# A hybrid decoder layer on one core: w_out loaded in two halves of its columns, and the first weight sums of the gated MLP on VectorE

## The chip, the cores and the metric

The kernel runs on one core of one Trainium2 chip. The metric is device time in microseconds, the median of three runs. The core has four engines that compute: TensorE (PE) for matmuls and transposes, VectorE (DVE), ScalarE (ACT) and GpSimd (POOL); SyncE (SP) issues the transfers. Each engine takes its instructions in the order in which they stand in its queue, and an instruction that waits holds all that stands behind it.

## What is computed

One layer on x of 1024 tokens by 1024 channels, in float32:

```python
h = rms_norm(x, norm_mix_pre)
proj = h @ w_in
a_out = spatial_gating(ua, va, ...)            # 256 channels
b_out = dilated_attention(qb, kb, vb, rel_bias) # 12 heads of 64
mix = concatenate([a_out, b_out], -1)
x = x + rms_norm(mix @ w_out, norm_mix_post)
h = rms_norm(x, norm_ffn_pre)
g = gelu(causal_dwconv(h @ w_gate, conv_w, conv_b))
y = (g * (h @ w_up)) @ w_down
x = x + rms_norm(y, norm_ffn_post)
```

The change touches the product with `w_out` (1024 by 1024), the end of the attention heads that stand before it, and the start of the gated MLP behind it.

## The kernel before

**Pairs of fp32r.** TensorE multiplies in a reduced float32 format. A value is therefore split into a high part (a cast) and a low part (value minus cast), and a product is three matmuls: high by high, low by high, high by low. `split(hi, lo, src, e1, e2)` makes the two parts, the cast on engine e1 (line 73 on ScalarE, line 77 on VectorE), the subtraction on e2 (line 78, VectorE or GpSimd).

**Heads.** The twelve heads run one after the other, each in four groups g. `qk_row` makes a row of scores (matmuls into `s`, the bias and minimum on VectorE, Exp on ScalarE at line 547, the scaling by 1/z on GpSimd at line 550). `tpv` transposes the rows (`pt`), takes them apart into `pth` (ScalarE, line 574) and `ptl` (VectorE, line 575), and multiplies them by V into `o`; `last` adds `o` into the mix tile `mixN` (lines 604, 605). Between these, `pump` takes matmuls from the deque `fill`, so that TensorE has work while the other engines prepare a group: in heads 0 to 9 they project Q and K of a later head (`proj_qk`), in the last head (h = 11) they are the first products with w_out.

**w_out.** `load_wo(k)` loads 128 rows of w_out (512 KB) into one of two raw buffers and splits them in two halves of 512 columns into `wohK` and `wolK`. The eight tiles are loaded during head 10 by `WO_AT`; the strings `WO_HI` and `WO_LO` name the engines of casts and subtractions. A raw buffer comes free when the subtractions on it are done. `mix_split` splits the eight 128x128 blocks of one token tile of the mix (`ms`). `wout_mm(i, ks, get)` gives the matmuls of token tile i into two PSUM banks, `y_i_0` for the left 512 columns and `y_i_1` for the right. In the last head the fill is tile 0 with blocks k = 0 to 6 (42 matmuls); block 7 follows when the head is done, then come tiles 1 to 4, 6, 5, 7 in the order `TO`.

**Norms.** `wout_end(i)` closes a tile: two squares with sums on ScalarE (line 725), a root on ScalarE (161), a step on GpSimd (166), scaling by g2 on VectorE (729), the sum with x (730), a square on ScalarE (733), a root (150), a step on GpSimd (154), and the scaling `xb` on VectorE (735). `h2_trans` transposes the result (`hT`, line 747). The transposes of a tile stand behind the y matmuls of the next tile in TensorE's queue.

**MLP.** The products with w_gate and w_up are in seven products of 2x2 blocks (Strassen's), with sums of weight blocks (`tsums`: four subtractions of 128x512) and of activations (`hs_sums`), each split again (`hs`, `wtg`, `wtu`). `HEAD` gives the order of the first three units, a = gate 0, b = up 0, c = gate 1: "1a 1b 2a 1c 2b 2c 4a 6a 6b 7a ...". `wsplit` is written three products ahead (`LOOK`). `tsums` before puts its first and last subtraction on GpSimd (lines 824 and 827), the others on VectorE (825, 826). `TO[7]` = 7 is transposed at j = 4. The scheduler orders instructions by the order of the code and their readiness; `tc.high_priority(400)` lets those in it go ahead.

Of the kernel before, what the change touches and what calls it, by code (L numbers as in the profile page):

```python
# [26 lines left out]
R = mybir.dt.float32r  # L27
# [8 lines left out]
KT = D // 128  # L36
HEADS = 12
# [15 lines left out]
WQK_HI = 'aa'  # L53
WO_HI = 'dadaddda'
WO_LO = 'pppppppd'
WO_AT = {0: (0, 1), 1: (), 2: (2, 3), 3: (4, 5), 4: (6, 7)}
# [6 lines left out]
def build(tc, x, g1, g2, g3, g4, w_in, ln_g, ln_b, sp_w, sp_b, rel, w_out, w_gate, w_up,  # L63
# [28 lines left out]
    with tc.manual_schedule(engines={ET.PE, ET.SP}), \  # L92
# [530 lines left out]

        def load_wo(k):
            r = raw("wo%d" % k)
            sp.dma_start(r, w_out[k * 128:(k + 1) * 128, :])
            wh = htile("woh%d" % k)
            wl = htile("wol%d" % k)
            for s in (slice(0, 512), slice(512, 1024)):
                split(wh[:, s], wl[:, s], r[:, s], ENG[WO_HI[k]], ENG[WO_LO[k]])  # L630
            WO.append((wh, wl))

# [8 lines left out]

        def wout_mm(i, ks, get):
            def mm(hf, k, j):
                def f():
                    if k == 0 and j == 0:
                        YP[i, hf] = get("y%d_%d" % (i, hf))
                    m = MS[i][1 if j == 2 else 0][:, k]
                    w = WO[k][1 if j == 1 else 0][:, hf * 512:(hf + 1) * 512]
                    pe.matmul(YP[i, hf], m, w, start=k == 0 and j == 0, stop=k == KT - 1 and j == 2)  # L649
                return f  # L650
            return [mm(hf, k, j) for k in ks for hf in range(2) for j in range(3)]

# [6 lines left out]
        for h in range(HEADS):  # L659
# [6 lines left out]
            if h == HEADS - 1:  # L666
                pump(len(fill))
                fill.extend(wout_mm(0, range(KT - 1), bD))
            for g in range(4):
# [16 lines left out]
                if g == 3 and h == HEADS - 2:  # L686
                    pump(len(fill))
                    for k in WO_AT[4]:
                        load_wo(k)
        pump(len(fill))  # L690
        last_pv()
        close_pool("ag")
        close_pool("ag2")
# [129 lines left out]
        def tsums(u):  # L823
            pool.tensor_sub(tw(u, 0), wblk(u, 0, 1), wblk(u, 0, 0))  # L824
            dve.tensor_sub(tw(u, 1), wblk(u, 1, 1), tw(u, 0))
            dve.tensor_sub(tw(u, 2), wblk(u, 1, 1), wblk(u, 0, 1))
            pool.tensor_sub(tw(u, 3), wblk(u, 1, 0), tw(u, 1))

# [286 lines left out]
        load_xb(1)  # L1115
        for f in wout_mm(0, [KT - 1], bD):
            f()
        wout_end(0)
        mt = mix_tiles(1)
        mix_split(1, mt[0], mt[1], range(KT))  # L1120
        for c in range(1, NT):
# [7 lines left out]
            if c == 6:  # L1129
# [3 lines left out]
                hs_sums(0, 2)  # L1133
            for f in wout_mm(i, range(KT), bS if c % 2 else bD):
                f()
            if c < 6:
                wout_end(i)
            else:
                with tc.high_priority(400):
                    wout_end(i)  # L1140
# [16 lines left out]
        for j, (u, n) in enumerate(SEQ):  # L1157
# [5 lines left out]
            if j == 1:  # L1163
                with tc.high_priority(400):
                    h2_trans(TO[NT - 2], bD)
                store_x1(TO[NT - 2])
                tsums(U[0])
                hs_sums(2, 3)
                hsplit(4, 0, 3)
# [4 lines left out]
            if j == 4:  # L1174
                with tc.high_priority(400):
                    h2_trans(NT - 1, bD)
                store_x1(NT - 1)
                hsplit(4, 3, 4)
                hs_sums(3, 4)
                hsplit(6, 3, 4)  # L1180
                hsplit(7, 3, 4)
                tsums(U[1])
                hsplit(5, 0, 4)
                hsplit(3, 0, 4)
# [104 lines left out]
```

## Time and profile before

| | before |
|---|---|
| device time, median of 3 runs | 1190.84 us (1188.72 to 1192.52) |
| the profiled execution | 1192.9 us |
| its span | 1191.2 us |
| TensorE busy | 1162.8 us (98%) |
| VectorE busy | 832.0 us (70%) |
| ScalarE busy | 593.1 us (50%) |
| GpSimd busy | 351.0 us (29%) |

Times in the rows are microseconds from the start of the span. TensorE is the engine that is nearly always busy; of its 28 us without work 10.9 lie between 400 and 600 us, where head 10 ends at about 431, head 11 at about 458, the products with w_out at about 550, and the MLP begins. Idle time of the other engines costs nothing in itself.

### The profile page before, as it was taken

The numbers are of one execution on the slowest core, as the hardware profiler recorded it, in microseconds if no ns is written. First come the engines' busy times: TensorE is split into PE (matmuls) and PEld (weight loads), VectorE is DVE, ScalarE is ACT, GpSimd is POOL, SyncE is SP. The second block draws the span as 40 slices with busy tenths as digits, with TensorE's granted clock in tenths as the row PEclk, the third lists the DMA queues.
The fourth block names the chain that finished last, engine by engine and source line by source line (L and its number), as shares of the span: only waits on it lengthen the run. The fifth ranks groups of instructions, "written<-read, shape, count | busy, mean of one in ns | idle before, by whom it ended". The sixth has DMA issues, their size and how long they took to land.

```text
span 1191.2 us, 16581 instructions
## 1 busy us (share of the span) xinstructions
PE 1162.8 (98%) x5697; PEld 975.0 (82%) x5697; DVE 832.0 (70%) x1553; ACT 593.1 (50%) x1233; POOL 351.0 (29%) x356
## 2 busy tenths in 40 slices
PE   8999999999999999998999999999999999999997
PEld 5889978888888878877788888888888888888885
DVE  6842157767777775467997778767777679679666
ACT  6522157676766665467534243433434245445642
POOL 2841023333334473224133313332233310000240
PEclk9999999999999999999999999999999999999999
DMA  5314033443234341341143313333243279334337
GB/s 196 104 47 113 2 83 73 103 108 83 74 78 110 86 131 72 103 164 53 36 133 97 106 65 130 123 108 89 80 133 97 85 279 370 114 98 120 113 108 245
DMA packets 107421, 134.31 MB, mean 113 GB/s; under 512 B 30780, under 2 KB 74312, under 8 KB 107337
## 3 DMA queue, kind: packets, MB, share of 16 engines
q1 hardware_dynamic: 105030, 131.15, 36.1%
q10 hardware_dynamic: 2306, 2.10, 0.5%
q8 instruction: 45, 0.74, 0.3%
q14 instruction: 40, 0.32, 0.1%
HBM read 98.30 MB, written 35.71 MB: 113 GB/s over the span
## 4 chain that ended last, share of the span: by engine, by line
PE 82%; issue 4%; ACT 4%; POOL 4%; DVE 4%; DMA 1%; DVEq 0%; POOLq 0%; ACTq 0%; SPq 0%
PE d L1015 15%; PE qk L498 10%; PE y L649 5%; PE o L592 4%; PE pt L570 4%; PE s L538 2%; PE s L539 2%; PE v L253 2%; PE Bu L876 2%; PE v L254 2%; PE v L255 2%; PE Bu L874 2%; PE Bu L875 2%; PE Au L876 2%; PE Cu L876 2%
## 5 line engine op out<-in xcount | busy, mean ns | idle before, releaser
L1015 PE MATMUL d<-t,s 128*128 128x512 f32 x924 | 210.4, 389 | 0.8 <-DVE t L78 0.8
L1015 PEld LDWEIGHTS d<-t,s 128*128 128x128 f32 x924 | 173.2, 188 | 37.8 <-DVE t L78 1.7
L550 POOL TENSOR_SCALAR row<-row,rz 128x128 f32<-128x128 f32 (+3 forms) x96 | 72.7, 757 | 208.3 <-DVE rz L549 190.7
L547 ACT ACTIVATE row<-row,nm 128x128 f32<-128x128 f32 (+3 forms) x96 | 74.4, 775 | 49.7 <-DVE nm L542 49.5
L575 DVE TENSOR_TENSOR ptl<-pt,pth 128x512 fp32r<-128x512 f32 (+1 forms) x120 | 75.7, 634 | 20.0 <-ACT pth L574 18.7
L649 PE MATMUL y<-woh,ms 128*128 128x512 f32 x256 | 82.8, 396 | 1.0 <-POOL ms L78 0.6
L574 ACT ACTIVATE pth<-pt 128x512 fp32r<-128x512 f32 (+1 forms) x120 | 65.9, 551 | 33.3 <-PE pt L570 31.9
L498 PE MATMUL qk<-hTh,wqh 128*128 128x512 f32 x192 | 81.0, 422 | 0.0
L73 ACT ACTIVATE s<-sf 128x512 fp32r<-128x512 f32 x77 | 48.2, 626 | 63.1 <-PE d L1015 26.3
L498 PE MATMUL qk<-hTl,wqh 128*128 128x512 f32 x192 | 78.7, 410 | 0.0
L498 PE MATMUL qk<-hTh,wql 128*128 128x512 f32 x192 | 76.7, 400 | 0.0
L78 DVE TENSOR_TENSOR s<-sf,s 128x512 fp32r<-128x512 f32 x77 | 57.1, 741 | 21.1 <-ACT s L73 21.0
L570 PE MATMUL pt<-ident,row 128*128 128x128 f32 x432 | 68.3, 275 | 1.1 <-POOL row L550 1.0
L73 ACT ACTIVATE wtg<-tg 128x512 fp32r<-128x512 f32 x44 | 27.4, 632 | 81.4 <-PE Cu L876 67.8
L1030 POOL TENSOR_TENSOR x<-x,g4t 128x512 f32<-128x512 f32 x12 | 18.0, 1516 | 163.4 <-ACT n4m L1040 133.5
L927 DVE SCALAR_TENSOR_TENSOR c<-G,cols,c 128x1023 f32<-128x1023 f32 (+1 forms) x44 | 57.7, 1327 | 6.7 <-ACT c L925 6.7
L542 DVE CUSTOM_DVE_ANT_0 row<-s,bias 128x384 f32<-128x384 f32 (+2 forms) x96 | 49.9, 520 | 17.8 <-PE s L539 12.4
L824 POOL TENSOR_TENSOR tu<-wu 128x512 f32<-128x512 f32 x11 | 16.9, 1537 | 153.6 <-PE Ag L876 74.5
L73 ACT ACTIVATE wtu<-tu 128x512 fp32r<-128x512 f32 x44 | 27.6, 630 | 63.9 <-PE Cg L876 50.8
L570 PEld LDWEIGHTS pt<-ident,row 128*128 128x128 f32 x432 | 51.2, 140 | 10.0 <-POOL row L550 2.0
L649 PEld LDWEIGHTS y<-woh,ms 128*128 128x128 f32 x256 | 47.9, 188 | 11.7 <-POOL ms L78 1.0
L592 PE MATMUL o<-ptl,V 128*128 128x256 f32 x240 | 49.1, 286 | 3.7 <-DVE ptl L575 3.4
(334 smaller groups left out, 3214.1 us busy)
## 6 DMA issues: line engine op xcount, KB each, us to landing
sf<-sD SPq DMA_DIRECT2D x77, 256.0 KB, 2.9
wu<-in_w_up SPq DMA_DIRECT2D x11, 1024.0 KB, 5.1
wd<-in_w_down SPq DMA_DIRECT2D x22, 512.0 KB, 6.9
wg<-in_w_gate SPq DMA_DIRECT2D x10, 1024.0 KB, 6.5
sD<-c SPq DMA_DIRECT2D x30, 256.0 KB, 6.4
gcop<-gd SPq DMA_DIRECT2D x12, 576.0 KB, 4.8
wqk<-in_w_in SPq DMA_DIRECT2D x24, 256.0 KB, 5.8
bias<-gcop SPq DMA_DIRECT2D x12, 512.0 KB, 3.9
```

Source lines behind the costliest of these rows:

```text
L73: act.activation(hi, src, AF.Copy)
L498: pe.matmul(st[hf], w, m, start=k == 0 and j == 0, stop=k == KT - 1 and j == 2)
L547: act.activation(t[:, :w], t[:, :w], AF.Exp, bias=nm, scale=-1.0, accum_out=z)
L550: pool.tensor_scalar(t[:, :w], t[:, :w], rz, 1.0, op0=OP.mult, op1=OP.mult)
L570: pe.transpose(p[:, a * 128:(a + 1) * 128], r[:, jj * 128:(jj + 1) * 128], ident)
L574: act.activation(hi[:, :n], p[:, :n], AF.Copy)
L575: dve.tensor_sub(lo[:, :n], p[:, :n], hi.bitcast(F)[:, :n])
L592: pe.matmul(ov, v, t[:, s], start=j == 0 and x == 0, stop=x == 1 and j == 2 * g + 1, skip_group_check=True)
L649: pe.matmul(YP[i, hf], m, w, start=k == 0 and j == 0, stop=k == KT - 1 and j == 2)
L876: pe.matmul(b, wl, hh, start=False, stop=last and k == 3, skip_group_check=True)
L927: dve.scalar_tensor_tensor(c[:, d:T], g[:, 0:T - d], col(2 - d, f), c[:, d:T], op0=OP.mult, op1=OP.add)
L1015: pe.matmul(b, l, r, start=first and n in FIRST and q == 0, stop=last and n in LAST and q == 2, skip_group_check=True)
```

## The change

`load_wo(k, hf)` loads and splits one half of the columns (256 KB). The left halves are loaded in head 10 in the places where whole tiles were; the right halves 0 to 3 behind group 3 of the last head in the code, 4 to 7 behind its last product. All casts of right halves are on ScalarE, the subtractions go to VectorE and GpSimd in turn. In the last head the fill is the left half of token tiles 0 and 1, k = 0 to 6 (42 matmuls again), so tile 1's mix is split there as well. Behind the head stand block 7 of both left halves, then the right half of tile 0, then that of tile 1. The weight sums of the first two units are made by VectorE alone; those of the first are moved to the last token tile's products, those of the second are left to the first `wsplit` that needs them. Three further edits: tile 5's norm (c = 5) is at high priority too, tile 2 takes one bank of each kind, and the hs splits at j = 4 are at high priority.

```diff
-WO_HI = 'dadaddda'
-WO_LO = 'pppppppd'
+WO_HI = 'dadaddda', 'aaaaaaaa'
+WO_LO = 'pppppppd', 'dpdpdpdp'
...
+        def load_wo(k, hf=0):
+
+            s = slice(hf * 512, (hf + 1) * 512)
+            r = raw("wo%d_%d" % (k, hf))
+            sp.dma_start(r[:, :512], w_out[k * 128:(k + 1) * 128, s])
+            if hf == 0:
+                WO.append((htile("woh%d" % k), htile("wol%d" % k)))
+            wh, wl = WO[k]
+            split(wh[:, s], wl[:, s], r[:, :512], ENG[WO_HI[hf][k]], ENG[WO_LO[hf][k]])
...
-            return [mm(hf, k, j) for k in ks for hf in range(2) for j in range(3)]
+            return [mm(hf, k, j) for k in ks for hf in hfs for j in range(3)]
...
             if h == HEADS - 1:
                 pump(len(fill))
-                fill.extend(wout_mm(0, range(KT - 1), bD))
+                m1 = [mtile("ms1_%d" % s, R).rearrange("p (k c) -> p k c", k=KT) for s in range(2)]
+                mix_split(1, m1[0], m1[1], range(KT - 1), (act, pool))
+                for i in range(2):
+                    fill.extend(wout_mm(i, range(KT - 1), bD, (0,)))
...
+                if g == 3 and h == HEADS - 1:
+                    for k in range(4):
+                        load_wo(k, 1)
         pump(len(fill))
         last_pv()
+        for k in range(4, KT):
+            load_wo(k, 1)
...
         def tsums(u):
-            pool.tensor_sub(tw(u, 0), wblk(u, 0, 1), wblk(u, 0, 0))
+            e = dve if u in U[:2] else pool
+            e.tensor_sub(tw(u, 0), wblk(u, 0, 1), wblk(u, 0, 0))
             dve.tensor_sub(tw(u, 1), wblk(u, 1, 1), tw(u, 0))
             dve.tensor_sub(tw(u, 2), wblk(u, 1, 1), wblk(u, 0, 1))
-            pool.tensor_sub(tw(u, 3), wblk(u, 1, 0), tw(u, 1))
+            e.tensor_sub(tw(u, 3), wblk(u, 1, 0), tw(u, 1))
...
-        for f in wout_mm(0, [KT - 1], bD):
+        mix_split(1, m1[0], m1[1], [KT - 1])
+        for i in range(2):
+            for f in wout_mm(i, [KT - 1], bD, (0,)):
+                f()
+        for f in wout_mm(0, range(KT), bS, (1,)):
             f()
         wout_end(0)
-        mt = mix_tiles(1)
-        mix_split(1, mt[0], mt[1], range(KT))
...
-            for f in wout_mm(i, range(KT), bS if c % 2 else bD):
+            if c == 7:
+                tsums(U[0])
+            for f in wout_mm(i, range(KT), (lambda nm: (bD if nm.endswith("_0") else bS)(nm)) if c == 2 else bS if c % 2 else bD, (1,) if c == 1 else (0, 1)):
                 f()
-            if c < 6:
+            if c < 5:
                 wout_end(i)
...
-                tsums(U[0])
...
-                hsplit(4, 3, 4)
-                hs_sums(3, 4)
-                hsplit(6, 3, 4)
-                hsplit(7, 3, 4)
-                tsums(U[1])
+                with tc.high_priority(400):
+                    hsplit(4, 3, 4)
+                    hs_sums(3, 4)
+                    hsplit(6, 3, 4)
+                    hsplit(7, 3, 4)
```

On ScalarE, in the middle of the last head (names carry head, group or row, and part: `row11_5` is score row 5 of head 11, `woh0` the high part of the first 128 rows of w_out), there stood before:

```order
478 L574 ACTIVATE pth11_1_0_5325<-pt11_1_0_5320 128x512
479 L73 ACTIVATE woh7_5226<-wo7_5224 128x512 x2
480 L73 ACTIVATE ms0_0_4858<-mix7_4897 128x128
481 L547 ACTIVATE row11_5_5296,z11_5_5307<-row11_5_5296,nm11_5_384_5305 128x768
482 L574 ACTIVATE pth11_1_1_5340<-pt11_1_1_5336 128x384
483 L604 ACTIVATE ot11_1_5388<-o11_1_5335 64x256
484 L547 ACTIVATE row11_6_5352,z11_6_5363<-row11_6_5352,nm11_6_384_5361 128x896
485 L574 ACTIVATE pth11_2_0_5396<-pt11_2_0_5391 128x512
```

and there stands now, in the same place:

```order
485 L73 ACTIVATE ms1_0_5216<-mix6_4219 128x128
486 L574 ACTIVATE pth11_1_0_5324<-pt11_1_0_5319 128x512
487 L73 ACTIVATE ms0_0_4858<-mix7_4893 128x128
488 L73 ACTIVATE ms1_0_5216<-mix7_4893 128x128
489 L574 ACTIVATE pth11_1_1_5339<-pt11_1_1_5335 128x384
490 L73 ACTIVATE woh0_4876<-wo0_1_5504 128x512
491 L547 ACTIVATE row11_5_5295,z11_5_5306<-row11_5_5295,nm11_5_384_5304 128x768
492 L73 ACTIVATE woh1_4882<-wo1_1_5508 128x512
493 L547 ACTIVATE row11_6_5351,z11_6_5362<-row11_6_5351,nm11_6_384_5360 128x896
494 L604 ACTIVATE ot11_1_5387<-o11_1_5334 64x256
495 L73 ACTIVATE woh2_5021<-wo2_1_5512 128x512
496 L574 ACTIVATE pth11_2_0_5395<-pt11_2_0_5390 128x512
```

Casts of right halves stand now between the Exps and the pth copies, and seven casts of ms1 ahead of pth11_1_0; further on, those of the sixth and seventh right half stand ahead of pth11_3_2, the eighth behind ot11_3.

On TensorE, behind the last head, there stood before:

```order
2255 L649 MATMUL y0_0_5269<-woh7_5226,ms0_0_4858 128x512
2256 L649 MATMUL y0_0_5269<-wol7_5227,ms0_0_4858 128x512
2257 L649 MATMUL y0_0_5269<-woh7_5226,ms0_1_4859 128x512
2258 L649 MATMUL y0_1_5273<-woh7_5226,ms0_0_4858 128x512
2259 L649 MATMUL y0_1_5273<-wol7_5227,ms0_0_4858 128x512
2260 L649 MATMUL y0_1_5273<-woh7_5226,ms0_1_4859 128x512
2261 L649 MATMUL y1_0_5589<-woh0_4876,ms1_0_5553 128x512
```

and there stands now:

```order
2255 L650 MATMUL y0_0_5269<-woh7_5212,ms0_0_4858 128x512
2256 L650 MATMUL y0_0_5269<-wol7_5213,ms0_0_4858 128x512
2257 L650 MATMUL y0_0_5269<-woh7_5212,ms0_1_4859 128x512
2258 L650 MATMUL y1_0_5401<-woh7_5212,ms1_0_5216 128x512
2259 L650 MATMUL y1_0_5401<-wol7_5213,ms1_0_5216 128x512
2260 L650 MATMUL y1_0_5401<-woh7_5212,ms1_1_5217 128x512
2261 L650 MATMUL y0_1_5567<-woh0_4876,ms0_0_4858 128x512
```

The transposes hT0 stand at 2309 in both. Before, 48 matmuls of tile 1 stood between the end of tile 0 and them; now 24 of tile 0's right half come first, and 24 of tile 1's right half stand between.

On VectorE, at the start of the MLP (`tu0` are the sums of unit b, `hs3` to `hs7` the split activations, `wtu0_6` the weights of product 6b), there stood before:

```order
908 L826 TENSOR_TENSOR tu0_1_6527<-wu0_6035 128x512
909 L78 TENSOR_TENSOR hs6_1_0_6435<-stg0_0_0_5659,hs6_0_0_6434 128x2x128
910 L791 TENSOR_TENSOR stg0_1_1_5671<-stg0_1_1_5671,stg0_0_1_5660 128x2x128
911 L78 TENSOR_TENSOR hs6_1_1_6439<-stg0_0_1_5660,hs6_0_1_6438 128x2x128
912 L78 TENSOR_TENSOR hs5_1_0_6531<-hsum0_6164,hs5_0_0_6530 128x1024
913 L78 TENSOR_TENSOR hs5_1_1_6535<-hsum1_6169,hs5_0_1_6534 128x1024
914 L78 TENSOR_TENSOR hs3_1_0_6539<-stg0_1_0_5670,hs3_0_0_6538 128x1024
915 L78 TENSOR_TENSOR wtu0_6_6558<-tu0_0_6524,wtu0_6_6558 128x512
916 L78 TENSOR_TENSOR hs3_1_1_6543<-stg0_1_1_5671,hs3_0_1_6542 128x1024
```

and there stands now:

```order
907 L78 TENSOR_TENSOR hs5_1_1_6545<-hsum1_6185,hs5_0_1_6544 128x1024
908 L78 TENSOR_TENSOR hs6_1_1_6455<-stg0_0_1_5676,hs6_0_1_6454 128x2x128
909 L834 TENSOR_TENSOR tu0_0_6568<-wu0_6051 128x512
910 L836 TENSOR_TENSOR tu0_1_6571<-wu0_6051 128x512
911 L78 TENSOR_TENSOR hs3_1_0_6549<-stg0_1_0_5686,hs3_0_0_6548 128x1024
912 L78 TENSOR_TENSOR hs3_1_1_6553<-stg0_1_1_5687,hs3_0_1_6552 128x1024
913 L835 TENSOR_TENSOR tu0_0_6568<-wu0_6051,tu0_0_6568 128x512
914 L906 TENSOR_TENSOR tmpg0_0_6390<-Bg0_6610,tmpg0_0_6390 128x512
915 L837 TENSOR_TENSOR tu0_1_6571<-wu0_6051,tu0_0_6568 128x512
916 L78 TENSOR_TENSOR wtu0_6_6574<-tu0_0_6568,wtu0_6_6574 128x512
```

All four sums of unit b now stand on VectorE directly ahead of the low part of wtu0_6, behind hs5; before, two stood on GpSimd and the other two at 902 and 908.

On SyncE the eight loads of right halves stand behind that of the last left half, ahead of the loads of xb0, g2t and xb1.

## Rows read from the trace of the kernel before

**Rows 1.** Windows: length, busy us (x instructions) of PE, PEld, DVE, ACT, POOL, PEclk, DMA, GB/s.

```profile
400.00:600.00 200.00, 189.14 (x936) 155.75 (x935) 137.51 (x296) 118.21 (x297) 70.18 (x82) 0.99 0.30 96
600.00:1150.00 550.00, 550.00 (x2427) 455.23 (x2426) 416.21 (x559) 231.39 (x372) 131.43 (x90) 1.00 0.41 131
```

**Rows 2.** TensorE's waits, 380 to 620 us: total, times, longest.

```profile
PE hT L747 <- ACT hs L73: 1.5, 1, 1.5
...
PE y L649 <- DVE Q L513: 0.4, 1, 0.4
PE pt L570 <- POOL row L550: 0.4, 1, 0.4
```

**Rows 3.** Timeline (start, us, operation, [idle before <-releaser]) of head 10, and a window.

```profile
430.96 0.43 DVE L77 CAST woh<-wo 128x512 fp32r<-128x512 f32 x1 [2.11 <-DMA wo<-in_w_out]
...
432.44 0.51 PE L592 MATMUL o<-ptl,V 128*128 128x256 f32 x2 [1.90 <-DVE ptl L575]
...
430.00:440.00 10.00, 7.71 (x46) 6.40 (x45) 7.30 (x20) 4.89 (x11) 4.70 (x6) 1.00 0.36 105
```

**Rows 4.** DMA issues: count, KB each, median us from issue to landing.

```profile
sf<-sD SPq DMA_DIRECT2D x77, 256.0 KB, 2.9
...
wo<-in_w_out SPq DMA_DIRECT2D x8, 512.0 KB, 4.8
```

**Rows 5.** Tile wo (ns min/median/max), then ScalarE's timeline in and behind the last head.

```profile
L78 POOL TENSOR_TENSOR wol<-wo,woh x14: 1279/1300/1438, 411.8 to 441.9; 128x512 fp32r<-128x512 f32 x14
...
L73 ACT ACTIVATE woh<-wo x6: 618/622/624, 413.3 to 442.1; 128x512 fp32r<-128x512 f32 x6
...
442.81 0.93 ACT L547 ACTIVATE row<-row,nm 128x768 f32<-128x768 f32 x1
...
455.79 0.60 ACT L574 ACTIVATE pth<-pt 128x512 fp32r<-128x512 f32 x1 [1.27 <-PE pt L570]
...
460.24 1.70 ACT L73 ACTIVATE ms<-mix 128x128 fp32r<-128x128 f32 x8
```

**Rows 6.** Timeline: a wait of tile 1, and steps of the norms of tiles 0 and 7.

```profile
462.24 0.50 PE L649 MATMUL y<-woh,ms 128*128 128x512 f32 x1 [0.62 <-POOL ms L78]
...
467.10 1.23 DVE L730 TENSOR_TENSOR yb<-yb,xb 128x1024 f32<-128x1024 f32 x1
470.51 0.75 DVE L735 TENSOR_SCALAR xb<-yb,n_0r 128x1024 f32<-128x1024 f32 x1 [2.19 <-POOL n_0r L154]
...
543.95 0.58 ACT L725 ACTIVATE yb<-y 128x512 f32<-128x512 f32 x1
...
544.65 0.29 ACT L161 ACTIVATE n_7m<-ssb,n_7m 128x1 f32<-128x1 f32 x1
...
545.02 0.55 POOL L166 TENSOR_TENSOR n_7r<-n_7m,half 128x1 f32<-128x1 f32 x1 [3.64 <-ACT n_7m L161]
...
545.60 1.41 DVE L729 SCALAR_TENSOR_TENSOR yb<-y,n_7r,g2t 128x512 f32<-128x512 f32 x2 [3.44 <-POOL n_7r L166]
```

**Rows 7.** Timeline of the start of the MLP, by engine, and a window.

```profile
549.49 6.04 POOL L827 TENSOR_TENSOR tg<-wg,tg 128x512 f32<-128x512 f32 x1 [2.67 <-DVE tg L825]
555.48 0.55 POOL L154 TENSOR_TENSOR n_7r<-n_7m,half 128x1 f32<-128x1 f32 x1
560.87 3.77 POOL L824 TENSOR_TENSOR tu<-wu 128x512 f32<-128x512 f32 x1 [4.83 <-PE Au L876]
...
556.07 0.76 DVE L735 TENSOR_SCALAR xb<-yb,n_7r 128x1024 f32<-128x1024 f32 x1 [1.70 <-POOL n_7r L154]
...
573.08 0.68 DVE L78 TENSOR_TENSOR wtu<-tu,wtu 128x512 fp32r<-128x512 f32 x1
...
565.76 0.50 PE L875 MATMUL Eg<-hs,wtg 128*128 128x512 f32 x1 [2.03 <-DVE hs L78]
...
573.81 0.50 PE L876 MATMUL Bu<-hs,wtu 128*128 128x512 f32 x1 [0.42 <-DVE wtu L78]
...
565.00:570.00 5.00, 4.24 (x13) 3.28 (x14) 5.00 (x11) 3.00 (x3) 1.31 (x1) 0.72 0.00 0
```

More of the change, by code (lines that the diff above doesn't have):

```diff
@@ L622, in build @@
         WO, MS = [], {}
[L624 to L631, printed above, removed]
+        def load_wo(k, hf=0):
[6 more added lines that the diff above has]
+            split(wh[:, s], wl[:, s], r[:, :512], ENG[WO_HI[hf][k]], ENG[WO_LO[hf][k]])
         def mix_split(i, mh, ml, ks, engs=None):
@@ L640, in build, with wout_mm @@
         YP = {}
-        def wout_mm(i, ks, get):
+        def wout_mm(i, ks, get, hfs=(0, 1)):
             def mm(hf, k, j):
```

## The prediction

> **What bounds the kernel now.** I read the busy time in two long stretches first [rows 1]. From 600 to 1150 us TensorE is busy 550.00 of 550.00 us: nothing that the change does to loads or to VectorE can be won or lost there, except by starting earlier or later. From 400 to 600 us it is busy 189.14 of 200, so 10.9 us of idle time lie in the stretch that the change touches; with some clock loss (below) that is the whole prize. The kernel is bound by TensorE, so each edit is priced as TensorE time: a wait that goes, a wait that comes, or a start that moves. The set of matmuls is the same before and after, and from 600 us on the order of all engines is the same. The matmul price is 550 us over 2427 matmuls, 0.227 us each [rows 1]. The second view is the list of TensorE's waits in 380 to 620 us [rows 2]; of what the change could remove it names 1.5 us ahead of hT7 (F says why) and 0.4 each for a score row and for the evacuation of head 11's Q. The longer ones are in the timelines below.
>
> **The change, part by part.** The sum is made against the profiled execution (1192.9 us, its span 1191.2), which lies 2.1 us above the median of the runs, 1190.84; I take 2.1 off at the end.
>
> **A. Head 10: only left halves are loaded and split.** VectorE stood 2.11 us for the sixth tile of w_out to land, and behind it in its queue stood the low part that TensorE wanted: 1.90 us of TensorE idle [rows 3]. With 256 KB in place of 512 KB the landing comes earlier: a 256 KB load in the trace takes 2.9 us to landing, the 512 KB of w_out 4.8 [rows 4], so the 2.11 us of VectorE are about covered, and the 1.90 goes. GpSimd has one low split of 1.30 us a tile [rows 5] where it had two, so the 0.4 for a score row [rows 2] goes as well. Against that, the cast of the first tile stands one step earlier on VectorE, and its load is queued right behind a 512 KB bias load; I take 0.8 us of new waiting for it, an estimate between zero and the 1.9 that the similar block cost. −1.9 −0.4 +0.8 = **−1.5** (−2.3 to −0.4).
>
> A rule speaks against counting so much for the halving. The Trainium skill, "DMA: Bandwidth & Descriptors", section "Anatomy of one DMA", gives every transfer about 2.0 us that don't depend on its size. The trace agrees in kind: its 2.9 us for 256 KB are more than half of the 4.8 for 512 KB, so halving buys 1.9 us and not 2.4.
>
> **B. Last head: the right halves come in.** Eight more loads, eight casts and eight low splits are put into the stretch 437 to 460 us. Only two raw buffers serve them, so each load waits for the low split of the load two before it: about 2.9 (landing) + 0.6 (cast) + 1.3 (split) [rows 4, 5] = 4.8 us a turn, two turns side by side, eight loads in about 20 us. All eight casts are on ScalarE, and ScalarE takes them in order: the cast of the first right half stands ahead of the Exp of row 5 (before at 442.81), the sixth and seventh ahead of the third pth of the last group (before at 455.79) [rows 5]. By the chain, loads six and seven land at about 458 to 460, so the queue stands there, and TensorE's last o products stand behind it, when only a few fill matmuls are left. Seven casts of tile 1's mix also stand ahead of the first pth of group 1: eight took 1.70 us [rows 5], so 1.5, with a w_out cast of 0.6 ahead of them; fill matmuls hide about 0.7 of that. TensorE: first o of group 1 waits +1.4; low part of group 2 behind a w_out split on VectorE +0.5; the last two o behind casts six and seven +1.9; the wait for the second bank (0.4, Q [rows 2]) goes, since both fill tiles' left halves use the first kind of bank as it comes free. **+3.4** (0 if the loads land in 2.2 us or the fill hides the casts; +6 if they land in 3.5 and more).
>
> **C.** The wait for tile 1's low mix on GpSimd at 462.24 [rows 6] goes, as tile 1 is split in the last head: **−0.6**.
>
> **D. Tile 0's norm is no longer covered.** Before, tile 0 was whole at the end of the fill and 48 matmuls of tile 1 stood between it and its transposes: 48 × 0.227 = 10.9 us. Now the right half of tile 0 is finished late, and only the 24 of tile 1's right half stand between: 5.4 us. The chain from a tile's last matmul to its transposes goes by the starts of its steps in [rows 6], tile 7's first: the second square starts at 543.95 (0.3 us behind the matmul, an estimate), the root 0.70 later at 544.65, GpSimd 0.37 later at 545.02, VectorE 0.58 later at 545.60; 1.41 for its two halves; then tile 0's rows, 3.41 from the sum with x at 467.10 to xb at 470.51, and 0.75 for xb, 0.1 to TensorE: 7.6 to 7.7 in all. So TensorE stands for 7.7 − 5.4 = **+2.3** (2.0 to 3.0). Nothing else of TensorE's stands between: its queue is in order, and the next tile's products are behind the transposes.
>
> **E.** Two weight sums of unit 0 on VectorE ahead of xb6, 0.68 us each, cover mostly by idle time there: **+0.2**.
>
> **F. Start of the MLP.** GpSimd's four sums were slow: 6.04 us for one (549.49), and n_7r had to wait for it until 555.48; 3.77 for another (560.87), behind which VectorE and then hs stood, and TensorE 2.03 us at 565.76 [rows 7]. On VectorE such a sum takes 0.68 us. So n_7r and hT7 come 3 us earlier and the waits of 1.5 and 2.0 go. But what is late next is the first Bu product (before at 573.81, behind the split of unit 1's sixth weight product at 573.08 [rows 7]). In the new order VectorE makes unit 1's sums only behind the splits of hs5 and the last piece of hs6, and that split stands behind both hs3 splits (1.2 us each), one tmpg and the last sum. VectorE had 17.0 us from xb7 (556.07) to that split with 1.2 of idle; it now has 17.0 − 1.2 + 4.5 (0.95 + 0.68 moved behind xb7, a sum 0.6, a hs3 split 1.2, tmpg 0.6, the last sum 0.5) = 20.3. It starts at about 552: from n_7r's first step at 545.02 the chain of D has 5.4 to xb7, 550.4, and VectorE's own queue, 1.6 of splits and sums ahead of it, makes 552. So the split starts at 572.3 to 573 in the old clock, 0.1 to 0.8 before it did; I take 0.6. The time won by hT7 is waited away in front of Bu. **−0.6** (−5.7, all of the waits and the clock loss, to +1).
>
> The rule that bears here: the Trainium skill, "GPSIMD Engine Reference", section "Key points", says that GpSimd shares its SBUF interfaces with VectorE, against VectorE instructions with two SBUF inputs, and that VectorE is about twice as fast at elementwise work. A GpSimd split of 1.30 us [rows 5] against 0.68 on VectorE [rows 7] agrees with the second part, and 6.04 and 3.77 for the same shape beside a busy VectorE agree with the first. By the rule alone F would be the whole −5.7; the order of VectorE's queue is why I don't take it.
>
> **G. The clock.** After the waits at 557 and 565.76 the granted clock was 0.72 in 565 to 570 us [rows 7], a mix of the two levels, 1.2 and 2.4 GHz: 13 matmuls took 4.24 us where 13 × 0.227 = 2.95, so 1.3 us lost. That loss lies ahead of Bu, in time that F counts as waited anyway. The new wait ahead of Bu is 3 to 4 us in one piece; I expect the same loss behind it: **+1.3** (0 to +1.7). After the 1.90 us of idle of A no loss is seen (granted clock 1.00 in 430 to 440 us [rows 3]); the 2.3 us of D may or may not bring one, 0 to 1.5, taken as 0.
>
> Sum: −1.5 + 3.4 − 0.6 + 2.3 + 0.2 − 0.6 + 1.3 = +4.5; 1192.9 + 4.5 = 1197.4 for a profiled execution, **1195.3** for the median.
>
> **Rivals.** (1) *The last head hides its loads*: the landings are short enough that no cast stops ScalarE; B is then 0 to +1, the sum about +1.5, the time 1192.3. For it: ScalarE was idle 1.27 us ahead of the row at 455.79, and DMA is lightly used (0.30 share [rows 1]). Against: two buffers only. (2) *Faster*: hs and the sums on VectorE fall better than I have laid them (idle VectorE time ahead of hs5 taken up by the sums), so that Bu follows without a wait; F is then −5.0 and G 0, B at +1.5 or so, the sum about −3.7, the time 1187; it decides when VectorE reaches unit 1's sums before about 566. By the Trainium skill's rule above it would be this one. (3) *More clock loss*: D's wait brings one too and loads land in 3.5 us; +1.5 and +2.6 more, 1199.5. (4) *The halves pay the fixed part twice without any use*: A gives nothing (2.9 us isn't early enough), −1.5 becomes 0, 1196.8; this lies within the forecast's own range.
>
> **How the numbers follow.** About 0.3% (3.6 us) is what a measurement of this kernel can tell from no change: faster below 1187.3, slower above 1194.4. Chances: forecast (with rival 4, 1193.5 to 1198) 0.50, of which 0.08 falls under 1194.4; rival 1 0.22, nearly all within 0.3%; rival 2 0.14, of which 0.10 below 1187.3; rival 3 0.14. Faster 0.11, same 0.31, slower 0.58. The range reaches from the slow end of rival 2, 1188, to rival 3, 1199.5.
>
> **What would show it.** In the profile after: no VectorE wait on a w_out load near 430 (A); ScalarE idle on a w_out load ahead of row 5's Exp and ahead of the third pth of the last group (B); TensorE idle 2 to 3 us ahead of the first hT (D); hT7 near 3 us earlier against the matmuls around it, and then one idle of 3 us or more ahead of Bu with a granted clock under 1 behind it (F, G). Wrong if ScalarE never stands on those loads (then rival 1), or if Bu doesn't wait (rival 2).

## The result and the profile after

| | before | after |
|---|---|---|
| device time, median | 1191.68 us (4 runs, 1188.72 to 1192.87) | 1201.28 us (4 runs, 1201.05 to 1206.69) |
| profiled execution (span) | 1192.9 us (1191.2) | 1206.69 us (1205.0) |
| TensorE busy | 1162.8 us | 1170.4 us |

The ratio is 1.0088, with a 95% interval of 1.0071 to 1.0105: slower by 0.9%, where +4.5 us, 0.4%, was forecast, and above the end of the range (1199.5). The direction and most of the places were right; the size was not.

The stretches of the profile after (columns as in [rows 1]; the first two lines answer to [rows 1], the others show the clock):

```profile
400.00:600.00 200.00, 184.04 (x890) 150.75 (x889) 129.98 (x274) 113.78 (x297) 54.74 (x78) 0.97 0.28 94
614.00:1164.00 550.00, 550.00 (x2428) 455.19 (x2427) 417.13 (x561) 233.45 (x377) 131.53 (x90) 1.00 0.40 129
460.00:465.00 5.00, 3.67 (x12) 3.09 (x13) 2.62 (x7) 2.50 (x5) 0.19 (x1) 0.58 0.72 244
465.00:470.00 5.00, 5.00 (x18) 3.99 (x17) 3.18 (x6) 1.67 (x7) 3.02 (x5) 0.74 0.31 123
480.00:485.00 5.00, 5.00 (x20) 4.10 (x21) 3.10 (x4) 3.00 (x13) 2.13 (x5) 0.66 0.15 60
```

The long stretch of products is unchanged: 550.00 of 550.00 us busy. Between 400 and 600 us TensorE did 890 matmuls where it had done 936, with 5 us more idle and a granted clock of 0.97 in place of 0.99. Both levels of the clock, 1.2 and 2.4 GHz, lie mixed in three of the five-us stretches; "half clock" below is the lower of them.

TensorE's gaps in the timeline of after, with what ended them:

```profile
442.91 0.50 PE L592 MATMUL o<-pth,V 128*128 128x256 f32 x2 [0.66 <-ACT pth L574]
...
461.28 0.79 PE L592 MATMUL o<-pth,V 128*128 128x256 f32 x2 [2.61 <-ACT pth L574]
...
479.95 1.07 PE L756 MATMUL hT<-ident,xb 128*128 128x128 f32 x8 [2.04 <-DVE xb L744]
...
542.42 1.09 PE L756 MATMUL hT<-ident,xb 128*128 128x128 f32 x8 [1.74 <-DVE xb L744]
...
582.71 0.50 PE L884 MATMUL Bu<-hs,wtu 128*128 128x512 f32 x1 [3.37 <-ACT wtu L73]
...
607.92 0.47 PE L884 MATMUL Bg<-hs,wtg 128*128 128x512 f32 x1 [1.02 <-DVE tmpg L906]
...
1183.73 13.49 PE L1025 MATMUL d<-t,s 128*128 128x512 f32 x50 [1.91 <-DVE t L78]
```

The first two are the last head (B of the prediction), the third is tile 0's norm without cover (D), the fourth E, the fifth F. The waits of [rows 3], [rows 6] and the 2.03 of [rows 7] are gone. For the fourth, sixth and seventh gap, the profile of before has these at the same matmuls:

```profile
531.66 1.09 PE L747 MATMUL hT<-ident,xb 128*128 128x128 f32 x8 [1.11 <-DVE xb L735]
...
596.44 0.47 PE L874 MATMUL Bg<-hs,wtg 128*128 128x512 f32 x1 [1.02 <-ACT wtg L73]
...
1170.94 0.97 PE L1015 MATMUL d<-t,s 128*128 128x512 f32 x3 [0.56 <-DVE t L78]
```

So E's cost is the step from 1.11 to 1.74 us, and the sixth gap is nothing new. The seventh, 0.56 before and 1.91 now, was in no step of the prediction.

**A ruler.** Every kernel here has 5697 matmuls, so the start of the n-th matmul can be set against that of the n-th matmul of before. The difference, counted from a matmul at 350 us, is the time lost or won up to that place. Places: the end of head 10; the middle of head 11; the end of head 11, just ahead of its last o products and so ahead of the 2.61 us wait of after; the last products before tile 0's transposes; behind those; behind the transposes of tile 6; behind the start of the MLP; 30 us from the end; the last products.

| kernel, first profile | h10 | h11 mid | h11 end | before hT0 | behind hT0 | behind hT6 | MLP | 1160 | end |
|---|---|---|---|---|---|---|---|---|---|
| after | −0.9 | +1.0 | +1.5 | +6.3 | +10.2 | +10.8 | +11.5 | +11.5 | +14.2 |
| after, second profile | −0.8 | +1.0 | +1.5 | +6.3 | +10.1 | +10.7 | +11.5 | +11.4 | +14.1 |
| before, second profile | −0.8 | −0.6 | −0.6 | −0.6 | −0.6 | −0.6 | −0.5 | −0.6 | +0.6 |
| x1_wout_only | −0.9 | +1.1 | +1.6 | +4.4 | +8.3 | +8.3 | +8.3 | +8.3 | +11.1 |
| x2_mlp_only | −1.2 | −0.8 | −0.8 | −0.8 | −0.8 | −0.1 | +1.1 | +1.0 | +4.2 |
| x3_four_raw | −0.9 | +0.9 | +4.9 | +3.8 | +6.1 | +6.7 | +7.4 | +7.4 | +10.0 |
| x4_ht0_late | −0.8 | +1.0 | +1.5 | +2.7 | +3.6 | +6.0 | +7.4 | +7.4 | +10.0 |
| x5_tsums_early | +1.0 | +2.8 | +3.3 | +7.3 | +11.2 | +11.9 | +8.1 | +8.1 | +10.6 |
| x6_no_right_loads | +3.8 | +5.4 | +6.1 | +5.0 | +7.2 | +7.9 | +8.3 | +8.2 | +9.0 |
| x9_no_right | −0.7 | +1.1 | +0.8 | −0.4 | +1.9 | +2.5 | +2.8 | +2.7 | +5.2 |
| x10_pool_casts | −0.8 | +0.3 | +6.6 | +13.0 | +13.1 | +13.7 | +14.5 | +14.5 | +17.0 |
| x8_before_sums_early | −0.4 | 0.0 | 0.0 | 0.0 | 0.0 | +0.7 | −3.1 | −3.2 | −2.6 |
| x11_pool_lo | −0.6 | −0.4 | −0.4 | −0.4 | −0.4 | +0.2 | −3.1 | −2.9 | +0.1 |

A difference between two lines that stays within 0.8 us says little: the two profiles of before differ by that at head 10 already.

### The profile page after: what moved, and what is told of

Its sections match the earlier page's. It is cut to its first block, busy times and chain, and to the rows that moved or that the text cites. A ratio compares the mean times of both kernels' runs of the same rounds, so it can differ in the third digit from the quotient of the medians.

```text
span 1205.0 us, 16584 instructions
## 1 busy us (share of the span) xinstructions
PE 1170.4 (97%) x5697; PEld 980.3 (81%) x5697; DVE 835.9 (69%) x1547; ACT 596.6 (50%) x1242; POOL 336.4 (28%) x353
## 4 chain that ended last, share of the span: by engine, by line
PE 84%; DVE 5%; ACT 4%; issue 2%; POOL 2%; DMA 2%; SPq 0%; DVEq 0%; POOLq 0%; ACTq 0%
PE d L1025 15%; PE qk L498 10%; PE y L650 5%; PE o L592 4%; PE pt L570 4%; PE s L538 2%; PE s L539 2%; PE Bu L886 2%; PE v L253 2%; PE Bu L884 2%; PE Bu L885 2%; PE v L254 2%; PE v L255 2%; PE Au L884 2%; PE Cu L884 2%
## 5 line engine op out<-in xcount | busy, mean ns | idle before, releaser
L650 PEld LDWEIGHTS y<-woh,ms 128*128 128x128 f32 x256 | 49.8, 195 | 10.2
L834 POOL TENSOR_TENSOR tu<-wu 128x512 f32<-128x512 f32 x10 | 13.2, 1318 | 148.7 <-PE Ag L886 89.8
L592 PEld LDWEIGHTS o<-pth,V 128*128 128x128 f32 x240 | 44.0, 190 | 12.4 <-ACT pth L574 4.4
```

Of the source, the lines that this page charges most:

```text
L592: pe.matmul(ov, v, t[:, s], start=j == 0 and x == 0, stop=x == 1 and j == 2 * g + 1, skip_group_check=True)
```

## Experiments

### The two halves of the change alone: x1_wout_only, x2_mlp_only

x1 keeps the w_out part and takes the MLP part back; x2 is the reverse. The core of x2 against before:

```diff
-            pool.tensor_sub(tw(u, 0), wblk(u, 0, 1), wblk(u, 0, 0))
+            e = dve if u in U[:2] else pool
+            e.tensor_sub(tw(u, 0), wblk(u, 0, 1), wblk(u, 0, 0))
...
+            if c == 7:
+                tsums(U[0])
```

> All of the w_out part of the change (halves, two tiles in the fill, right halves in the last head), with the weight sums and priorities of the MLP as before. My theory, that the loss is made before the first transposes (tile 0's stand 8.5 us later in the profile after, 10.1 with the clock loss behind them) and that the MLP part is about even: 7 to 9 us over before, about 1199. Rival, that the sums on VectorE cost about half of it: about 4 us over before, 1195 to 1196.

> Only the MLP part (sums of the first two units on VectorE, their places, the two priorities), with w_out as before. My theory: -0.8 at the first Bu, +0.6 at the transposes of tile 6, +1.0 at a later Bg, clock losses as before: within 0 to +1.5 us of before, 1191 to 1193. Rival: +4 to +5 us, 1195 to 1196. A third, that the wins in front of hT7 come through once the w_out part is gone: -3 us, 1188.

x1 measured 1.0081 of before (1.0063 to 1.0100), x2 1.0017 (1.0003 to 1.0030). The w_out part carries nearly all of the loss: x1 lies 10.1 us over the median of before in its call (7 to 9 were forecast), x2 2.5 (0 to 1.5). In the ruler x2 loses 0.7 at hT6 and 1.2 more in the start of the MLP. The third branch, that hT7's win comes through alone, is refuted: its waits were replaced, not removed.

### What in the last head costs: x9_no_right, x6_no_right_loads, x3_four_raw, x10_pool_casts

x9 leaves out the right halves altogether, x6 their loads only, x3 puts two right halves into one raw buffer, x10 puts their casts on GpSimd.

```diff
 # x9
-                    w = WO[k][1 if j == 1 else 0][:, hf * 512:(hf + 1) * 512]
+                    w = WO[k][1 if j == 1 else 0][:, :512]
...
-                        load_wo(k, 1)
 # x6
+            if hf:
+                r = mixT[0]
 # x3
+                if k % 2 == 0:
+                    RAWP[k // 2] = raw("wo%d_%d" % (k, hf))
+                r = RAWP[k // 2][:, (k % 2) * 512:(k % 2 + 1) * 512]
 # x10
-WO_HI = 'dadaddda', 'aaaaaaaa'
+WO_HI = 'dadaddda', 'pppppppp'
```

> The changed kernel without the right halves: no loads, casts or splits of them; the matmuls of the right columns read the left ones (the right columns of w_out are left out of the result). ScalarE's order is that of the changed kernel without the eight casts. If right halves in the queue are the cost of the last head: the shift against before ahead of tile 0's transposes falls from +2.7 (without clock loss) to about -1, 1196 to 1197.5. If it is the seven casts and low splits of tile 1's mix that now stand in the head: it stays above +1, 1199 or more.

> The changed kernel without the eight loads of right halves: the casts and low splits read a tile of the mix that is resident, so the work on ScalarE, VectorE and GpSimd stays and every wait for these loads is gone (the right half of w_out is left out of the result). If the waits for loads are the cost of the last head, the shift at the end of the head against before falls from +3.8 (without clock loss) to within 1 us, and the half clock at 461 us doesn't show: 5 to 7 us under the changed kernel, about 1195. If the queue work is the cost, less than 2 us.

> The changed kernel, with two right halves in one raw buffer, so that four right halves can be on the way and a load waits for a split four places back. If the wait of ScalarE on the fifth to seventh load (2.1 + 1.6 us in the profile after) is what makes the last head 4.7 us longer, most of it goes: 3 to 5 us under the changed kernel, 1197 to 1198.5. If only the work of casts and mix splits counts, under 1 us of gain, about 1201.

> The changed kernel with the eight casts of right halves on GpSimd in place of ScalarE; the loads stay. If ScalarE standing on a load ahead of pth and Exp is the cost, the 2.6 us wait of TensorE for pth goes, and 2 to 4 us with it, 1197.5 to 1199.5. If GpSimd then stands on the loads ahead of the row scalings, the wait for row takes its place: no gain, 1200 to 1202.

Measured against before: x9 1.0040 (1.0021 to 1.0060), x6 1.0068 (1.0045 to 1.0092), x3 1.0068 (1.0047 to 1.0089), x10 1.0144 (1.0124 to 1.0163); x6 was timed twice only. x9 came out close to its first branch, x10 slower than both of its branches, x3 and x6 between theirs.

First the queue that the prediction named. ScalarE's timeline of after, in the last head:

```profile
440.86 1.51 ACT L73 ACTIVATE ms<-mix 128x128 fp32r<-128x128 f32 x7
442.28 0.58 ACT L574 ACTIVATE pth<-pt 128x512 fp32r<-128x512 f32 x1
...
453.16 0.63 ACT L73 ACTIVATE woh<-wo 128x512 fp32r<-128x512 f32 x1 [0.45 <-DMA wo<-in_w_out]
...
457.85 0.63 ACT L73 ACTIVATE woh<-wo 128x512 fp32r<-128x512 f32 x1 [2.11 <-DMA wo<-in_w_out]
460.11 0.63 ACT L73 ACTIVATE woh<-wo 128x512 fp32r<-128x512 f32 x1 [1.63 <-DMA wo<-in_w_out]
460.65 0.96 ACT L574 ACTIVATE pth<-pt 128x512 fp32r<-128x512 f32 x2
```

Loads six and seven are waited for at 457.85 and 460.11 (458 to 460 was forecast from two buffers and a turn of 4.8 us), and the pth that TensorE wants at 461.28 stands behind both. x9, without the right halves, reaches the transposes of tile 0 at −0.4; x4, whose last head is that of after but which had no half clock there, at +2.7; after at +6.3. So the right halves cost 3.1 us of waits, and in the profiles of after, where the granted clock fell to half behind the wait, 3.6 more (0.8 of it a longer wait: in x4 loads six and seven came together). The rest of the last head, which x9 keeps, is +1.5 from the end of head 10 to that of head 11, the seven casts of ms1 (1.4 was forecast), and then −1.2 for the wait at 462.24 of [rows 6] and what followed it.

Is it the landings that cost, or the casts and splits themselves? For this wait the profile of after answers. The wait is for a pth, and these rows are the pth copies ahead of it on ScalarE and the transposes on TensorE that it reads:

```profile
454.65 1.09 ACT L574 ACTIVATE pth<-pt 128x512 fp32r<-128x512 f32 x2
...
456.57 0.60 PE L570 MATMUL pt<-ident,row 128*128 128x128 f32 x4
```

ScalarE was free at 455.74, and that pth could not start before 457.17. Two casts of 0.63 us fit into these 1.43 us. It started at 460.65, as ScalarE stood 2.11 and 1.63 us for landings. By these rows the landings made the wait of 2.61 us, and the work of the two casts alone would have made none; up to there, by the ruler, the right halves had cost 0.7 us (after +1.5, x9 +0.8). That is worked out from the rows and not run: none of the next three edits separates the two, because each also changed the order of the queues.

In x6 nothing is loaded for the right halves, and the place ahead of tile 0's transposes is reached at +5.0, not under +1. But the scheduler put seven of the eight casts into head 10 or ahead of it and the eighth at 440.50, so that the stretch in question has none; +3.8 stands at the end of head 10 already. TensorE's gaps in x6, in head 10 and in head 11:

```profile
431.50 0.47 PE L592 MATMUL o<-pth,V 128*128 128x256 f32 x2 [1.99 <-DVE mix L605]
...
451.01 0.55 PE L570 MATMUL pt<-ident,row 128*128 128x128 f32 x3 [0.79 <-POOL row L550]
```

In x3 four right halves are on the way at a time, and their landings took longer: the five recorded for w_out 2.6 to 4.3 us, where after has 2.6 to 2.9. Three casts now stand ahead of an earlier pth, and the third still waits for its load. ScalarE's rows and TensorE's gap in x3:

```profile
452.05 1.21 ACT L73 ACTIVATE woh<-wo 128x512 fp32r<-128x512 f32 x2
454.77 0.63 ACT L73 ACTIVATE woh<-wo 128x512 fp32r<-128x512 f32 x1 [1.52 <-DMA wo<-in_w_out]
...
455.83 0.45 PE L592 MATMUL o<-pth,V 128*128 128x256 f32 x2 [2.15 <-ACT pth L574]
```

In x10 a cast takes 1.49 us on GpSimd (0.63 on ScalarE), GpSimd stands on the later loads for 1.37, 3.45 and 3.60 us, and the waits move to its row scalings and to the right halves themselves. TensorE's gaps there:

```profile
447.86 0.55 PE L570 MATMUL pt<-ident,row 128*128 128x128 f32 x3 [2.82 <-POOL row L550]
...
471.39 0.49 PE L650 MATMUL y<-woh,ms 128*128 128x512 f32 x1 [1.90 <-POOL woh L75]
...
474.26 0.79 PE L650 MATMUL y<-wol,ms 128*128 128x512 f32 x1 [2.38 <-POOL wol L78]
```

Ahead of tile 0's transposes x3 is 4.2 us later than x9, x6 5.4, after 6.7 and x10 13.4, each with a stretch of half clock in it, against 3.1 for x4, which has none. So the right halves cost TensorE time in every place and on either engine that was tried, most on GpSimd.

### Tile 0's transposes later: x4_ht0_late

```diff
-                h2_trans(TO[c - 1], bP)
+                if c > 1:
+                    if c == 2:
+                        h2_trans(TO[0], bP)
+                    h2_trans(TO[c - 1], bP)
```

> The changed kernel, with the transposes of tile 0 put behind tile 2's products (72 matmuls cover its norm in place of 24). My theory, that the 2.0 us wait ahead of them and the half clock behind it (1.6 us) are both bought by the short cover: 3 to 3.6 us under the changed kernel, about 1198. Rival, that the wait only moves on to the next tile's transposes: about 1201, as the changed kernel.

1.0083 of before (1.0052 to 1.0115), so no gain over after: my theory fell. The 2.04 us wait is gone, but the transposes of two tiles now stand in a row, and their copies out of PSUM on ScalarE are late. TensorE's gaps in x4:

```profile
487.53 0.66 PE L756 MATMUL hT<-ident,xb 128*128 128x128 f32 x4 [1.81 <-ACT stg L761]
488.56 0.66 PE L756 MATMUL hT<-ident,xb 128*128 128x128 f32 x4 [0.38 <-ACT stg L761]
```

1.81 + 0.38 = 2.19 us in place of 2.04. The ruler has +2.7 before and +5.3 behind both tiles (the +6.0 of the table has E in it), 2.6 us for the two where x9 has 2.3. So this edit moved the wait and did not remove it; what did shrink in x4's one profile, the half clock of 1.6 us behind it, does not show in the median.

### The sums at another time: x5_tsums_early, x8_before_sums_early, x11_pool_lo

x5 is after with one line, x8 is x2 with the same line, x11 is x8 with some low splits on GpSimd.

```diff
 # x5, x8: at j == 1, ahead of the last tile's norm
+                tsums(U[1])
 # x11
-            split(hv, lv, src, act, dve)
+            split(hv, lv, src, act, pool if u in U[:2] and n in (4, 5, 7) else dve)
```

> The changed kernel, with the weight sums of unit b made where those of unit a were before (ahead of the last tile's norm on VectorE, in idle time), not behind the hs5 splits. My theory: the wait of 3.4 + 0.35 us ahead of Bu shrinks below 1 us and the half clock behind it (1.7 us) goes: 4 to 5.5 us under the changed kernel, 1196 to 1197. Rival, that VectorE is simply full there and the splits of hs3 come as late as the sums did: less than 1.5 us, about 1200.

> The kernel before with the sums of both first units on VectorE and made early, in its idle time ahead of the last tile's norm; w_out as before. VectorE's chain from xb7 to the sixth product of unit b is the bound there (my theory): 3 to 4.5 us under before, 1188.5 to 1190. If the waits there are replaced by others and by half clock, as with the sums late (+0.17% measured): within 1 us of before, 1192 to 1194.

> The kernel before with the early sums on VectorE (0.9982 of before, measured) and with the low splits of the fourth, fifth and seventh products of units a and b on GpSimd, which is idle there. If VectorE is what bounds the start of the MLP, the waits of 0.9, 1.1 and 1.0 us that are left shrink and 1 to 3 us more are won, 1188 to 1190. If GpSimd's splits (1.3 us alone, 3.8 and 6.0 seen beside VectorE) come too late, it is the same or slower, 1191 to 1193.

Against before: x5 1.0056 (1.0036 to 1.0077), x8 0.9982 (0.9971 to 0.9993), x11 0.9985 (0.9974 to 0.9997). VectorE's timeline of after shows why the place matters:

```profile
577.77 0.69 DVE L834 TENSOR_TENSOR tu<-wu 128x512 f32<-128x512 f32 x1
578.37 0.69 DVE L836 TENSOR_TENSOR tu<-wu 128x512 f32<-128x512 f32 x1
578.97 2.36 DVE L78 TENSOR_TENSOR hs<-stg,hs 128x1024 fp32r<-128x1024 f32 x2
581.24 0.69 DVE L835 TENSOR_TENSOR tu<-wu,tu 128x512 f32<-128x512 f32 x1
...
583.04 0.69 DVE L78 TENSOR_TENSOR wtu<-tu,wtu 128x512 fp32r<-128x512 f32 x1
```

No idle stands ahead of any of them: VectorE is full, and TensorE's Bu waits for them through ScalarE's cast of `wtu`. Made early, the same sums fall into idle time of VectorE: its wait for tile 7's n_7r, 3.44 us in [rows 6], is 1.33 in x8:

```profile
544.80 1.41 DVE L729 SCALAR_TENSOR_TENSOR yb<-y,n_7r,g2t 128x512 f32<-128x512 f32 x2 [1.33 <-POOL n_7r L166]
```

The stretch behind hT6 to the MLP mark turns from +0.7 (after) into −3.8 (x5: +11.9 to +8.1) and −3.8 (x8: +0.7 to −3.1). TensorE's gaps in x8 in this stretch:

```profile
564.85 0.50 PE L876 MATMUL Bg<-hs,wtg 128*128 128x512 f32 x1 [0.92 <-DVE hs L78]
569.20 0.50 PE L877 MATMUL Bu<-hs,wtu 128*128 128x512 f32 x1 [1.10 <-DVE wtu L78]
...
591.83 0.47 PE L875 MATMUL Bg<-hs,wtg 128*128 128x512 f32 x1 [1.01 <-DVE tmpg L897]
```

x8 is faster than both kernels by the interval (2.3 us under before's median of that call, 1191.13 against 1193.43), though by less than 0.3% and by less than the 3 to 4.5 us of its theory. x5, 3.8 us under after by the two ratios, also falls a little short of its 4 to 5.5. Handing six splits to GpSimd (x11) adds nothing: the mark stays at −3.1.

### Second profiles: before_again, after_again

> The kernel before, unchanged, for a second profile of it. In the profile after and in four variants TensorE waits 1.9 to 2.4 us for the last split t of the last product with w_down, some 20 us from the end, with the clock at half behind it, 2.6 to 3.2 us in all; the first profile of before shows 0.56 + 0.24 us there. If that is a cost of the change, the second profile shows under 1 us again; if it is scatter in how x1d and sD land there, about 2 us.

> The changed kernel, unchanged, for a second profile: its first profiled execution was 5 us above its other runs. By the sum of the steps: the same waits (last head +4.7, tile 0's transposes +2.3, start of the MLP +1 to +1.5 against before), with fewer stretches at half clock than the four of the first profile; the sixth right half landing with the fifth, as in the profiles of two variants, would take 1 to 2 us more off. 1199 to 1203.

The second profile of after repeats the first to 0.1 us at every place of the ruler, with the same three half-clock stretches between 400 and 600 us. So its 1205.13 us are no accident of one execution. The timed executions of after without a profile (1201.05 to 1201.49) lie 3.6 to 5.6 us lower, at a mean clock of 0.993 to 0.994 in place of 0.990 and 0.991. The missing share of the clock, times the span, is 2.4 to 4.8 us less there, which would fit fewer or shorter half-clock stretches, but no trace of them is there to show it. Before has 0.996 in its first profile and 0.992 to 0.999, in the middle 0.995, in 46 other executions. By the same estimate the profile of after misses about 7 us more of the clock than that of before, and its timed runs (0.993 to 0.994 against 0.995 to 0.996) only 1 to 4 us more, out of the 9.6 that they are slower.

The second profile of before shows two things. TensorE's gaps in it:

```profile
563.91 0.50 PE L875 MATMUL Eg<-hs,wtg 128*128 128x512 f32 x1 [2.03 <-DVE hs L78]
...
571.97 0.50 PE L876 MATMUL Bu<-hs,wtu 128*128 128x512 f32 x1 [1.39 <-DVE wtu L78]
594.61 0.47 PE L874 MATMUL Bg<-hs,wtg 128*128 128x512 f32 x1 [1.01 <-ACT wtg L73]
...
1170.21 0.96 PE L1015 MATMUL d<-t,s 128*128 128x512 f32 x3 [1.72 <-DVE t L78]
```

There was no half clock at 567 us this time, and TensorE gained nothing: it waited 1.39 in place of 0.42 us at Bu (the 1.01 at the later Bg is in both), and the ruler stays at −0.5. So VectorE sets the pace ahead of Bu, with half clock or without. And the wait near the end was 1.72 us, where the first profile had 0.56: what the profiles of after lost in the last 30 us (+2.7) is in part scatter. It goes from 0 to 3.2 us over these kernels, and x8 (+0.6) and x11 (+3.0) lie near its ends though nothing there differs between them.

## Why the prediction was wrong

**A: right sign, too much.** −1.5 forecast, −0.9 measured at the end of head 10, with 0.8 us of scatter (the second profile of before has a wait of 1.13 where the first has 1.90). The load came down to 2.6 us, as the DMA rows of after have it (answering to [rows 4]; the 4.8 there is the middle of only two recorded landings, 3.8 and 5.7 us, and the 2.6 that of five, 2.6 to 2.9):

```profile
wo<-in_w_out SPq DMA_DIRECT2D x16, 256.0 KB, 2.6
```

and the 1.90 wait is gone (0.62 us ahead of a pth at 429.65 came in its stead), but the first left half makes VectorE wait at its new place, as forecast (0.8), and the score row's wait did not go but came earlier. VectorE and TensorE in after:

```profile
410.39 0.43 DVE L77 CAST woh<-wo 128x512 fp32r<-128x512 f32 x1 [0.77 <-DMA wo<-in_w_out]
...
411.27 0.44 PE L538 MATMUL s<-Kh,Q 128*128 128x384 f32 x1 [0.82 <-DVE nm L542]
412.91 0.55 PE L570 MATMUL pt<-ident,row 128*128 128x128 f32 x3 [0.49 <-POOL row L550]
```

The Trainium skill, "DMA: Bandwidth & Descriptors", section "Anatomy of one DMA", has about 2.0 us of a transfer independent of its size, for transfers that GpSimd issues; the prediction took it for every transfer, and these are issued by SyncE. By it, an estimate, 0.6 of the 2.6 us for 256 KB would depend on the size, and 2.8 of the 4.8 for 512 KB [rows 4], far more than twice as much. So the two medians do not agree with it together; halving bought 2.2 us between them.

**B and C: right mechanism, mostly the right places.** The sum of A, B and C was +1.3. Without a half clock it measured +2.7 (x4), 0.8 more from the head and 0.6 from A. The forecast chain of two buffers put loads six and seven within half a microsecond of where they were waited for; the eight loads took 20.0 us, from 440.14, as forecast. One sign did not come: ScalarE did not stand on a load ahead of row 5's Exp (the cast at 443.53 follows without idle time), only on loads five to seven.

**D: right.** +2.3 forecast; 2.04 us of wait, +2.3 in the ruler (x9: −0.4 to +1.9).

**E: short. F: right.** E measured +0.6 to +0.7 for +0.2; it was charged to the sums ahead of xb6, and x1, without them, has 0.0 there. F was −0.6 forecast; hT7 came 1.7 us earlier by the ruler (near 3 forecast), and Bu waited 3.37 us in one piece, as forecast (3 to 4). F and G together were +0.7, and from behind hT6 to the MLP mark after has +0.7.

**G: the failed step.** G charged one stretch of half clock, 1.3 us, behind Bu, put it at 0 behind D ("may or may not"), and did not look for it behind the wait in the last head. Behind Bu it came and was sized well. TensorE's rows there, the first and the last of nine products in a row:

```profile
583.79 0.79 PE L886 MATMUL Bu<-hs,wtu 128*128 128x512 f32 x1 [0.35 <-DVE wtu L78]
...
587.23 0.40 PE L885 MATMUL Bu<-hs,wtu 128*128 128x512 f32 x1
```

Eight steps take 3.44 us where 8 × 0.227 = 1.8: 1.6 us lost, and TensorE waits for nothing more until 607.92, where before has the same wait. What failed is that it was charged only there. Measured in the profile: about 2.8 us behind the 2.61 us wait at 461 (after +6.3, x4 +2.7, 0.8 of that a longer wait), and 1.6 behind the 2.04 us wait at 480 (3.9 from +6.3 to +10.2, where x9 has 2.3 with the same wait at full clock). So the clock cost 6.0 us in place of 1.3.

**Not in the prediction at all:** the last 30 us. "From 600 us on ... nothing can be won or lost" was read from 600 to 1150 us; the forecast did not look at the last 40, where before's own profile has 0.8 us of waits and the profiles of after 1.9, with the half clock behind it.

By the first profile: forecast +4.5, measured +13.8 in the span. The difference of 9.3 is 2.8 and 1.6 of clock behind two waits, 0.6 of A, 0.8 + 0.8 of the last head (the second for load seven alone), 2.7 at the end, 0.4 of E; 9.7 in all, and 0.4 is what the ruler (+14.2) differs from the span by.

The medians lie 9.6 us apart, 5.1 more than forecast. No run without a profile has a trace, so how these 5.1 divide stays open. By the mean clocks above, an estimate, 1 to 4 us of the 9.6 are clock and 6 to 9 are waits, for which A to F had 3.2: so in these runs A, the last head, E and the end, each sized short or left out, weigh about as much as G or more.

Of the rivals, the first (the last head hides its loads) and the second (faster) are refuted by the waits at 457.85 to 461.28 and at 582.71. The third, more clock loss and later loads, comes nearest; it was given 0.14 and ended at 1199.5. Its clock loss came, and one more; of its later loads only the seventh did, cast 4.7 us after its issue (455.43 to 460.11). Two sums of the prediction do not come out: rival 2's terms give −3.1 and not −3.7, so 1187.7, and F's bound of −5.7 has 1.5 + 2.0 + 0.4 + 1.3 = 5.2 in its waits and clock. The forecast uses neither.

## What to carry to other kernels

Where TensorE is nearly always busy, a new wait of about 2 us should be charged with the risk of a half-clock stretch behind it, at each place and not once: here 1.6 us behind 2.04, 2.8 behind 2.61 and 1.6 behind 3.37 us of waiting. Where another engine sets the pace, as VectorE does ahead of Bu in before, the stretch cost nothing (the two profiles of before). Two casts, 1.3 us together, would have fitted into ScalarE's idle time ahead of a pth, but in an ordered queue a cast that waits for its load holds the pth too. A norm that two tiles' worth of columns covered was not covered by half as many. And before moving work to a faster engine, look where that engine is idle: the same four sums cost 0.7 (after) and 1.2 us (x2) behind the splits and won 3.8 when made 28 us earlier.

## What the runs showed that was not expected

The clock repeats in part. Both profiles of after have half clock at the same three places between 400 and 600 us, and all eight profiles with a wait of 3.37 or 3.38 us ahead of Bu (after twice, x2, x3, x4, x6, x9, x10) have it there. The two profiles of before differ (granted 0.72 in 565 to 570 us in the first, 1.00 in the second). The wait of 2.04 us ahead of tile 0's transposes stands in seven profiles: behind it the clock fell in after (twice), x1 and x5, and stayed full in x3, x6 and x9. A row of x9 and the stretch behind it (columns as in [rows 1]):

```profile
473.30 1.06 PE L751 MATMUL hT<-ident,xb 128*128 128x128 f32 x8 [2.04 <-DVE xb L739]
475.00:480.00 5.00, 5.00 (x24) 4.11 (x23) 2.63 (x3) 2.70 (x8) 0.71 (x2) 1.00 0.20 79
```

After idle times of 1.90 us (before, 430.5) and 0.95 + 0.89 us (x4, 459 and 461) no half clock was seen, while x1 with 1.02 + 0.87 us at the same place had it. So the length of one wait does not decide it alone; what does is not shown here.
